# A hybrid attention and S5 block on one core: which weight matmuls stand beside which vector work, and the S5 scan on one engine

## Chip, core and metric

The kernel runs on one core of a Trainium2 chip. The metric is the device time of one execution in microseconds (us), as the median of the runs shown; the core is the only one, so its span is the execution but for what lies around it.

## What is computed

One decoder layer on 1024 tokens of width 1024, in float32:

```python
h = rmsnorm(x, norm_mix_pre)
q, k, v, u, g_attn, g_ssm = split(h @ w_in)     # 512, 128, 128, 512, 1024, 1024 columns
y_attn = sliding_window_attention(q, k, v, sinks, rel_bias) @ w_attn_branch
z = gelu(s5_ssm(u, lam, log_dt, b, c, d_skip))
z = z * sigmoid(z @ w_glu)
y_ssm = z @ w_ssm_branch
merged = sigmoid(g_attn) * y_attn + sigmoid(g_ssm) * y_ssm
x = x + rmsnorm(merged @ w_out, norm_mix_post)
h = rmsnorm(x, norm_mlp_pre)
x = x + rmsnorm(square(relu(h @ w_ff_in)) @ w_ff_out, norm_mlp_post)
```

The attention has 8 query heads on 2 key heads, blocks of 128 tokens with a band of 256 keys. The S5 part has 32 groups of 16 channels, each with a complex diagonal state of 64: `state = a * state + B u`, `y = Re(C state) + d u`, a scan along the sequence.

## The kernel before

**Number format.** Each float32 matmul is made of three: every operand is split into a high half (rounded by a copy on ScalarE) and a low half (`source - high`, on VectorE), and `mm3` (lines 184 to 190) issues high x high, high x low and low x high into one PSUM bank. One call of `proj_halves` (345) makes a 128x512 output tile from 8 such terms in two parts of 12 matmuls, with a `yield` between: such a part is what the text calls a step.

**Weights.** `WeightQueue` (45 to 121) loads raw weights in the order of the list in `weights` (209), as tiles of 128x2048 in two buffers, each two pieces of 1024. `pump` issues the high half of a piece (line 170), `flush` its low half (line 172) and the next loads. Three split pieces fit.

**Attention** (561) is a software pipeline over 16 half blocks in 20 iterations: iteration i issues the scores of half i (`a_scores`, with a maximum on VectorE), the softmax behind it (`a_softmax`: four Exp on ScalarE, line 523), transposes and splits for half i-2 (`a_trans`), the product with V for half i-3 (`a_pv`, copy at 556). At the end of an iteration come steps of a filler that keeps TensorE busy: one, and two in iterations 8, 11, 14, 15 and 16, so 24 in all. The filler is `u_proj` (813; 16 steps, u written to HBM as `ud`) and then the first 8 steps of `stage1` (956): for each of 16 tiles two steps of the gate g_attn, a sigmoid on ScalarE (972), one step of attention times w_attn_branch, their product on VectorE (985), written to HBM as `md`.

**Side work.** After attention the loop over the rest of stage1 calls `tick(11)` after each step (192 to 202): it plays pieces of a side generator, each with a cost, until the credit is spent or a piece says "wait". Side work is first `ssm_tables` (632): about a hundred small VectorE operations (recorded, so that all have line 42) for the exponentials and powers of a, the tables Vs (half of it on GpSimd), GW and four quarters of Q, with transposes (782) and small matmuls (765), written to HBM as `w1d`, `qd` and `kd`. Then `ssm` (833): `load1` reads `w1d` and `ud` back (lines 843, 846), `inputs` multiplies (864), the scan runs over state tiles F of 2x8x128, one half of the channels on VectorE and the other on GpSimd:

```python
v.tensor_tensor(out=t1, in0=src, in1=gb, op=ALU.mult)              # 877, src and dst: every 8th element
v.tensor_tensor(out=t2[:, 0], in0=src[:, 1], in1=g(2), op=ALU.mult)
v.tensor_tensor(out=t2[:, 1], in0=src[:, 0], in1=g(1), op=ALU.mult)
v.tensor_tensor(out=t1, in0=t1, in1=t2, op=ALU.add)
v.tensor_tensor(out=dst, in0=dst, in1=t1, op=ALU.add)              # 881
```

That is one `macc` (870); the scan has 18 (`scan`, 883). `stack` (895) moves halves of the partitions with three copies each (lines 902 to 904), `load2` (848) reads Q and T (from `qd`, `kd`; T by eight transfers, line 854), `outputs` (907) multiplies (916, 917), applies gelu (920 to 926) and writes z to HBM as `zd` in eight transfers per pair of tiles (932).

**Behind it.** `gates` (1023) makes the 16 tiles of sigmoid(g_ssm) into SBUF in 32 steps, still with ticks; before step 25 the side work is drained and `glu` (989) begins to load `zd`. Then glu's products, `stage2` (1036: branch times gates, `md` read back), `mix_out` (1120: w_out in three passes, norm) and `mlp`. The order is that of `run` (1294); nothing is reordered by a scheduler. Each engine takes its instructions in the order in which they are issued, and SP issues nearly all transfers.

Of the kernel before, what the change touches and what calls it, by code (L numbers as in the profile page):

```python
# [15 lines left out]
D = 1024  # L16
# [28 lines left out]
class WeightQueue:  # L45


    RAW, HL = 2, 3

    def __init__(self, blk, raws):  # L50
        self.blk = blk
        self.raws = raws
# [7 lines left out]
        self.halves = []  # L60

    def load(self, n=RAW):
        while self.in_use < n and self.n_load < len(self.raws):
            src, shape, own = self.raws[self.n_load]
            raw = self.blk.rawp.tile([P, 2048], F32, tag="raw", name="raw")
            n_pieces = src.shape[1] // 1024
            if self.n_load < 2:

                for i in range(n_pieces):
                    cs = slice(i * 1024, (i + 1) * 1024)  # L70
                    self.halves.append((raw[:, cs], src[:, cs]))
                self.load_half()
            else:
                self.blk.nc.sync.dma_start(out=raw[:, 0:n_pieces * 1024], in_=src)
            self.loaded.append((raw, [(i, shape, own[i]) for i in range(n_pieces)]))
            self.n_load += 1
            self.in_use += 1

    def load_half(self):
        out, src = self.halves.pop(0)  # L80
        self.blk.nc.sync.dma_start(out=out, in_=src)

    def pump(self, n=99):

        self.flush()
        while self.loaded and n:
            n -= 1
            raw, pieces = self.loaded[0]
            i, shape, own = pieces[0]
            if not own and self.live + self.ready_ring >= self.HL:  # L90
                break
            pieces.pop(0)
            last = not pieces
            if last:
                self.loaded.pop(0)
            src = raw[:, i * 1024:(i + 1) * 1024]
# [5 lines left out]
            self.pending.append((lo, last))  # L102

    def flush(self):
        for lo, last in self.pending:
            lo()
            self.in_use -= last
        self.pending = []
        self.load()
# [14 lines left out]
class Block:  # L124
    def __init__(self, ctx, tc, I, out):
# [3 lines left out]
        self.b16 = pool("b16", 6)  # L129
        self.r8 = pool("r8", 6)  # L130
        self.r4 = pool("r4", 3)
        self.t2 = pool("t2", 5)
        self.rawp = pool("raw", 2)
# [75 lines left out]
    def weights(self):  # L209
# [25 lines left out]
        return out + [ff2(NC - 1, keep(self.r, (0, 1)))]  # L235


    def consts(self):
# [8 lines left out]
        self.ones = c.tile([P, P], F32, name="ones")  # L247
# [38 lines left out]
    def x_load(self, q):  # L286
        nc, I = self.nc, self.I
        x, xt = self.r([2, D]), self.r([8, 256])
# [4 lines left out]
        if q == 0:  # L293
            nc.sync.dma_start(out=xt[:, 0:4], in_=I["xt"][q, :, 0:4])
            self.wq.load(1)
            self.wq.load_half()
# [90 lines left out]

    def qkv(self):
        nc = self.nc
        self.lo_eng = self.nc.gpsimd  # L390
        self.xq, self.xdiag = {}, {}
# [4 lines left out]
        self.wq.load_half()  # L396
# [13 lines left out]
        self.qa = (self.big([8, G, P]), self.big([8, G, P]))  # L410
# [8 lines left out]
        for qt in range(4):  # L419
# [6 lines left out]
            for n, (g, k, p) in enumerate(seq):  # L426
# [9 lines left out]
                if n == (32 if qt else 31) and qt + 1 < 4:  # L436
# [4 lines left out]
                    if qt == 2:  # L441
                        for g_ in range(3):
                            self.q_evac(early[g_], g_, 0)
            if qt == 3:
                self.lo_eng = None
            if qt == 1:
                early = ps
            if qt == 3:
                for g in range(3):
                    self.q_evac(ps[g], g, 1)  # L450
                    self.wq.done()
                    self.wq.pump()
        piece = self.wq.get()
        for h in range(2):
            ps = self.proj(piece, h)
            self.q_evac(ps, 3, h)
# [25 lines left out]
    def table_loads(self):  # L482
        self.tabA, self.tabB = self.r([2048]), self.r([2048])
# [77 lines left out]
    def attention(self, filler):  # L561
# [9 lines left out]
        for i in range(len(halves) + 4):  # L571
# [60 lines left out]
    def ssm_tables(self):  # L632
# [18 lines left out]
        self.GW = self.const.tile([P, 3, 11, 16], F32, name="GW")  # L651
# [61 lines left out]
        def powers(r_, i_, frm, k, to, m):  # L713
# [3 lines left out]
        powers(pr, pi, 1, 1, 2, 1)  # L717
        powers(pr, pi, 1, 2, 3, 2)
        powers(pr, pi, 1, 4, 5, 4)
# [4 lines left out]
        bb = lambda c: BB[:, c].unsqueeze(2).to_broadcast([P, 16, 8, 16])  # L724
        a = (pw4(0, 0, 16, 0, 8), pw4(1, 0, 16, 0, 8))
        T_ = [self.r([16, 8, 16]) for _ in range(2)]
        Vs = [self.r([16, 8, 16]) for _ in range(2)]
        self.cmul(nc.gpsimd, Vs[0], None, a, (bb(0), bb(1)), (T_[0], T_[0]))
        half = lambda v_, i: v_[:, 8 * i:8 * i + 8]
        for i in range(2):  # L730
            self.cmul(v, None, half(Vs[1], i), [half(x, i) for x in a], (half(bb(0), i), half(bb(1), i)), (None, half(T_[1], i)))
        yield from play(5)
# [4 lines left out]
        powers(gr, gi, 0, 0, 1, 1)  # L737
        powers(gr, gi, 0, 1, 2, 2)
        powers(gr, gi, 0, 3, 4, 4)
        for i in (8, 9, 10):  # L740
            powers(gr, gi, i - 1, i - 1, i, 1)
# [35 lines left out]
        def v_trans(ri, hf):  # L777
            pss = []
            for b in range(2):
                ps = self.ps()  # L780
                for k in range(4):
                    nc.tensor.transpose(ps[:, k * P:(k + 1) * P], Vs[ri][:, 8 * hf + 4 * b + k].rearrange("p t c -> p (t c)"), self.ident)
                pss.append(ps)
            return pss

        def v_out(ri, hf, pss):
            W = self.r([8, P])
            for b in range(2):
                nc.scalar.activation(out=W[:, 4 * b:4 * b + 4, :], in_=pss[b].rearrange("p (k s) -> p k s", k=4), func=AF.Copy)
            nc.sync.dma_start(out=self.w1d[hf, :, ri], in_=W)  # L790

        for q4 in range(4):
# [3 lines left out]
            Q = [self.q([4, 9, 16]) for _ in range(2)]  # L796
# [4 lines left out]
            yield from play(3)  # L801
# [6 lines left out]
            pss = v_trans(1 - q4 // 2, q4 % 2)  # L808
            yield "wait"
            kernel_out(q4, ps)  # L810
            v_out(1 - q4 // 2, q4 % 2, pss)

    def u_proj(self):
        nc = self.nc
        self.ud = self.dram.tile([SW, 8, P], F32, name="ud")
        for cp in range(2):
            ut = self.r([2, 8, P])
            for ci in range(2):
                piece = self.wq.get()
                for h in range(2):  # L820
                    for i, ps in enumerate(self.proj_halves(piece, h)):
                        if i == 1:
                            if h:
                                self.wq.done()
                                self.wq.pump()
                            nc.scalar.activation(out=ut[:, ci, :, 64 * h:64 * h + 64], in_=ps.rearrange("p (k j) -> p j k", j=8), func=AF.Copy)
                            if h:
                                c0 = cp * 256 + ci * P
                                nc.sync.dma_start(out=self.ud[c0:c0 + P], in_=ut[:, ci])
                        yield  # L830


    def ssm(self):
# [4 lines left out]
        xT, W1, F, T, Q = {}, {}, {}, {}, {}  # L838
# [17 lines left out]
        def inputs(hf):  # L856
            F[hf] = self.r([2, 8, P])
            nc.gpsimd.memset(F[hf][:, :, :, 0:1], 0.0)
# [537 lines left out]
```

## Time and profile before

| | us |
|---|---|
| three runs | 1364.54, 1367.31, 1368.42 (median 1367.31) |
| the profiled execution | 1364.96 |
| its span | 1363.2 |
| TensorE (PE) busy | 1293.4 (95%) |
| VectorE (DVE) busy | 778.8 (57%) |
| ScalarE (ACT) busy | 440.7 (32%) |
| GpSimd (POOL) busy | 209.7 (15%) |

How to read the rows: a row of busy time by stretch has the stretch, its length, then busy us and number of instructions of PE, PEld (weight loads), DVE, ACT and POOL, the granted TensorE clock (1.00 is 2.4 GHz, 0.50 is 1.2 GHz), the share of DMA time and GB/s. A row of a group has line, engine, operation, output<-input, shapes, number, then busy us, mean ns of one, and the idle time before them with what ended it. A row of the waits has who waited for whom, us in total, times, longest. A row of a timeline or of the chain has start, length, what. Matmuls overlap: two of 128x512 that follow each other start 0.227 us apart though each shows 0.39.

### The profile page before, as it was taken

The numbers are of one execution on the slowest core, as the hardware profiler recorded it, in microseconds if no ns is written. First come the engines' busy times: TensorE is split into PE (matmuls) and PEld (weight loads), VectorE is DVE, ScalarE is ACT, GpSimd is POOL, SyncE is SP. The second block draws the span as 40 slices with busy tenths as digits, with TensorE's granted clock in tenths as the row PEclk, the third lists the DMA queues.
The fourth block names the chain that finished last, engine by engine and source line by source line (L and its number), as shares of the span: only waits on it lengthen the run. The fifth ranks groups of instructions, "written<-read, shape, count | busy, mean of one in ns | idle before, by whom it ended". The sixth has DMA issues, their size and how long they took to land.

```text
span 1363.2 us, 15530 instructions
## 1 busy us (share of the span) xinstructions
PE 1293.4 (95%) x6144; PEld 1077.4 (79%) x6144; DVE 778.8 (57%) x1355; ACT 440.7 (32%) x774; POOL 209.7 (15%) x179
## 2 busy tenths in 40 slices
PE   8999999789749999998999999999999999999997
PEld 8988888677548778876788888888888888888886
DVE  5857869734982367467842554445544454445556
ACT  4557762212102253355543111211212111221132
POOL 1003214004970005152400000000000000000014
PEclk9999999898879999998999999999999999999999
DMA  8111021488105543455501010110011110110142
GB/s 340 48 62 63 32 93 57 130 199 171 47 31 120 127 155 124 154 186 185 186 31 62 31 62 32 62 62 31 33 61 62 49 45 31 63 62 31 49 180 96
DMA packets 42329, 124.22 MB, mean 91 GB/s; under 512 B 3856, under 2 KB 21008, under 8 KB 33552
## 3 DMA queue, kind: packets, MB, share of 16 engines
q1 hardware_dynamic: 42256, 123.22, 28.3%
q8 instruction: 48, 0.79, 0.2%
q14 instruction: 25, 0.20, 0.1%
HBM read 101.75 MB, written 21.46 MB: 90 GB/s over the span
## 4 chain that ended last, share of the span: by engine, by line
PE 73%; DVE 14%; ACT 5%; DMA 4%; issue 3%; SPq 1%; POOL 0%; DVEq 0%; ACTq 0%; POOLq 0%
PE ps L189 21%; PE ps L190 21%; PE ps L188 21%; DVE lo L172 2%; DMA r<-ud 1%; DVE r L42 1%; PE ps L1142 1%; PE ps L1143 1%; PE ps L1141 1%; DVE b L178 1%; DVE r L880 1%; ACT r L523 1%; DVE r L881 1%; DVE r L877 1%; DVE r L178 1%
## 5 line engine op out<-in xcount | busy, mean ns | idle before, releaser
L190 PE MATMUL ps<-b,lo 128*128 128x512 f32 x976 | 383.4, 393 | 17.7 <-DVE lo L172 17.7
L188 PE MATMUL ps<-b,hi 128*128 128x512 f32 x976 | 385.8, 395 | 1.3 <-ACT b L177 1.3
L189 PE MATMUL ps<-b,hi 128*128 128x512 f32 x976 | 383.1, 393 | 0.9 <-DVE b L178 0.9
L190 PEld LDWEIGHTS ps<-b,lo 128*128 128x128 f32 x976 | 185.1, 190 | 57.5 <-DVE lo L172 18.7
L170 ACT ACTIVATE hi<-raw 128x1024 fp32r<-128x1024 f32 x124 | 129.0, 1051 | 288.4 <-PE ps L190 236.9
L188 PEld LDWEIGHTS ps<-b,hi 128*128 128x128 f32 x976 | 185.4, 190 | 39.8 <-ACT b L177 1.9
L189 PEld LDWEIGHTS ps<-b,hi 128*128 128x128 f32 x976 | 185.0, 190 | 39.7 <-DVE b L178 1.8
L172 DVE TENSOR_TENSOR lo<-raw,hi 128x1024 fp32r<-128x1024 f32 x122 | 155.2, 1284 | 101.7 <-ACT hi L170 91.6
L1235 DVE TENSOR_TENSOR b<-b,ps 128x512 f32<-128x512 f32 x208 | 139.5, 686 | 98.9 <-PE ps L190 98.9
L190 PE MATMUL ps<-hi,r 128*128 128x512 f32 (+1 forms) x482 | 187.1, 388 | 0.0
L189 PE MATMUL ps<-lo,r 128*128 128x512 f32 (+1 forms) x482 | 187.1, 388 | 0.0
L188 PE MATMUL ps<-hi,r 128*128 128x512 f32 (+1 forms) x482 | 187.1, 388 | 0.0
L1176 DVE TENSOR_TENSOR t<-t 128x512 f32<-128x512 f32 x64 | 44.3, 692 | 163.9 <-ACT t L1175 163.9
L1289 POOL TENSOR_TENSOR t<-b,r 128x512 f32<-128x512 f32 (+1 forms) x17 | 20.5, 1227 | 663.8 <-DVE b L1286 663.8
L188 PEld LDWEIGHTS ps<-hi,r 128*128 128x128 f32 x482 | 90.5, 188 | 18.7
L189 PEld LDWEIGHTS ps<-lo,r 128*128 128x128 f32 x482 | 90.5, 188 | 18.7
L190 PEld LDWEIGHTS ps<-hi,r 128*128 128x128 f32 x482 | 90.5, 188 | 18.6
L1175 ACT ACTIVATE t<-ps 128x512 f32<-128x512 f32 x64 | 38.2, 597 | 189.7 <-PE ps L190 189.7
L178 DVE TENSOR_TENSOR r<-t,r 128x512 fp32r<-128x512 f32 x64 | 44.3, 693 | 44.8 <-ACT r L177 44.8
L177 ACT ACTIVATE r<-t 128x512 fp32r<-128x512 f32 x64 | 40.5, 633 | 49.9 <-DVE t L1176 48.9
L1142 PE MATMUL ps<-lo,b 128*128 128x512 f32 x128 | 51.5, 402 | 3.8 <-DVE lo L172 3.6
L1141 PE MATMUL ps<-hi,b 128*128 128x512 f32 x128 | 51.4, 402 | 1.7 <-DVE b L178 1.0
(198 smaller groups left out, 1550.1 us busy)
## 6 DMA issues: line engine op xcount, KB each, us to landing
raw<-in_ff_dram SPq DMA_DIRECT2D x32, 1024.0 KB, 4.9
raw<-in_wout_dram SPq DMA_DIRECT2D x12, 1024.0 KB, 4.9
raw<-in_win_dram SPq DMA_DIRECT2D x11, 1024.0 KB, 4.9
r<-in_x_dram SPq DMA_DIRECT2D x16, 512.0 KB, 7.3
md<-t SPq DMA_DIRECT2D x16, 256.0 KB, 2.0
raw<-in_wsb_dram SPq DMA_DIRECT2D x4, 1024.0 KB, 6.7
r<-md SPq DMA_DIRECT2D x4, 1024.0 KB, 8.2
x1d<-r SPq DMA_DIRECT2D x8, 512.0 KB, 6.0
```

The costliest lines, as they stand in the source:

```text
L170: nc.scalar.activation(out=hi, in_=src, func=AF.Copy)
L172: return (hi, lo), lambda: eng.tensor_tensor(out=lo, in0=src, in1=hi.bitcast(F32), op=ALU.subtract)
L177: nc.scalar.activation(out=hi, in_=src, func=AF.Copy)
L178: (eng or nc.vector).tensor_tensor(out=lo, in0=src, in1=hi.bitcast(F32), op=ALU.subtract)
L188: self.nc.tensor.matmul(ps, lhsT=ah, rhs=bh, start=first and i == 0, stop=False)
L189: self.nc.tensor.matmul(ps, lhsT=ah, rhs=bl, start=False, stop=False)
L190: self.nc.tensor.matmul(ps, lhsT=al, rhs=bh, start=False, stop=last and i == n - 1)
L1141: nc.tensor.matmul(ac[c], lhsT=a, rhs=wh[:, cs], start=k == 0, stop=False)
L1142: nc.tensor.matmul(ac[c], lhsT=a, rhs=wl[:, cs], start=False, stop=False)
L1175: nc.scalar.activation(out=rl, in_=ps, func=AF.Relu)
L1176: nc.vector.tensor_tensor(out=rl, in0=rl, in1=rl, op=ALU.mult)
L1235: nc.vector.tensor_tensor(out=a, in0=a, in1=ps, op=ALU.add)
```

## The change

In the order of the kernel:

- `weights`: the two slabs of u come first, the slabs of the SSM gates before those of stage1. Weights are loaded as pieces of 128x1024 in three buffers.
- `qkv`: the three pieces projected beside the norm of x are u's; the fourth u piece and the four q pieces follow with `tick(11)` after each of their 20 steps. Beside them the new generator `ssm_inputs_tables` plays the first part of the tables: the exponentials, powers, and Vs, now wholly on VectorE in two halves, with its transposes and `w1d`. Then `drain`.
- Attention has as filler 24 steps of `gates(range(6))` (12 tiles, whose sigmoids go to HBM as `sd`), then stage1; two steps in iterations 4 to 16, one in the others up to 18: 32 steps. From iteration 2 on `tick(8)` plays the second part of the tables (GW and Q). Then `drain`.
- The other 40 steps of stage1 have `ssm` beside them with `tick(11)`, then `drain`, with no step between. F is one tile of both halves, and one scan on VectorE does both (18 maccs of double width); all four `stack` steps are on VectorE.
- glu begins to load after that `drain`; `gates(range(6, 8))` makes the last four tiles beside it (8 steps).
- `stage2` reads `sd` back beside `md`. Pools: 7 large tiles for 6, 5 of 8 KB for 6, 3 raw for 2, 2 for Q; `ones` shares GW's tile.

```diff
-        win = lambda i: (I["win"][i], col, keep(self.r, (1,)) if i == 1 else none)
-        out = [win(i) for i in range(5)]
+        win = lambda i: (I["win"][i], col, keep(self.r, (1,)) if i == 4 else none)
+        out = [win(i) for i in (3, 4, 0, 1, 2)] + [win(9 + dp) for dp in range(3)]
         for dp in range(4):
             out += [(I["wab"][dp], half, none), win(5 + dp)]
-        out += [win(9 + dp) for dp in range(4)]
+        out.append(win(12))
...
+        self.side = [self.ssm_inputs_tables()]
+        for h, ps in self.proj_ticks(self.wq.get(), 11):
+            self.u_evac(ps, 3, h)
+        self.qa = (self.big([8, G, P]), self.big([8, G, P]))
+        for g in range(4):
+            piece = self.wq.get()
+            for h, ps in self.proj_ticks(piece, 11):
+                if h:
+                    self.wq.done()
+                    self.wq.pump()
+                self.q_evac(ps, g, h)
+        self.drain()
...
-            for _ in range(1 + (i in (8, 11, 14, 15, 16)) if i < 19 else 0):
+            for _ in range(1 + (4 <= i < 17) if i < 19 else 0):
                 next(filler, None)
+            if i >= 2:
+                self.tick(8)
...
+        for hf in range(2):
+            qs = slice(8 * hf, 8 * hf + 8)
...
+            self.cmul(v, Vs[0][:, qs], Vs[1][:, qs], a, (bb(0), bb(1)), (T_[:, 0], T_[:, 1]))
+            yield from play(6)
+            yield "wait"
...
-        def macc(hf, dst, src, i, n):
-
-            v = nc.gpsimd if hf else nc.vector
-            qs = slice(8 * hf, 8 * hf + 8)
-            g = lambda c: self.GW[:, c, i, qs].unsqueeze(2).to_broadcast([P, 8, n])
...
+        def macc(dst, src, i, n):
+
+            g = lambda c: self.GW[:, c, i].unsqueeze(2).to_broadcast([P, 16, n])
...
-                macc(hf, Fv[:, :, :, :, b], Fv[:, :, :, :, b - 1], 0, 16)
-                yield "wait"
+                macc(Fv[:, :, :, :, b], Fv[:, :, :, :, b - 1], 0, 16)
+                yield 14
...
         load2(0)
-        for step in (scan(1), stack(1)):
-            for _ in step:
-                pass
-        for _ in scan(0):
-            yield 8
+        yield from scan()
         yield from stack(0)
+        yield from stack(1)
         yield "wait"
         yield from outputs(0)
         load2(1)
...
-                self.nc.scalar.activation(out=self.sig[h][:, d], in_=ps, func=AF.Sigmoid)
+                sg = self.t([512])
+                nc.scalar.activation(out=sg, in_=ps, func=AF.Sigmoid)
+                nc.sync.dma_start(out=self.sd[d * P:(d + 1) * P, 512 * h:512 * h + 512], in_=sg)
...
             s1 = self.stage1()
-            self.attention(itertools.chain(self.u_proj(), s1))
-            self.table_loads()
-            self.side += [self.ssm_tables(), self.ssm()]
-            for i, _ in enumerate(s1):
+            self.side = [self.ssm_tables()]
+            self.attention(itertools.chain(self.gates(range(6)), s1))
+            self.drain()
+            self.side = [self.ssm()]
+            for _ in s1:
                 self.tick(11)
+            self.drain()
             glu = self.glu()
-            for i, g in enumerate(self.gates()):
-                self.tick(11)
-                if i == 24:
-                    self.drain()
-                    next(glu)
-                if i == 28:
+            next(glu)
+            for i, _ in enumerate(self.gates(range(6, 8))):
+                if i == 4:
                     next(glu)
```

## Rows read from the trace of the kernel before

**Rows 1.** Busy time by stretch: section A, then section B.

```profile
87.50:198.50 111.00, 110.39 (x604) 93.15 (x602) 84.94 (x263) 81.73 (x226) 28.63 (x16) 1.00 0.15 50
198.50:480.40 281.90, 237.16 (x1218) 196.99 (x1216) 171.41 (x323) 58.78 (x86) 89.33 (x105) 0.92 0.46 113
```

**Rows 2.** Busy time by stretch: slices of 20 us.

```profile
240.00:260.00 20.00, 12.32 (x60) 9.49 (x59) 15.47 (x61) 3.22 (x5) 0.19 (x1) 0.74 0.30 99
...
380.00:400.00 20.00, 2.79 (x14) 2.28 (x13) 19.45 (x27) 0.00 (x0) 18.67 (x27) 0.64 0.15 52
...
500.00:520.00 20.00, 18.32 (x73) 14.46 (x72) 12.96 (x15) 8.86 (x12) 4.64 (x4) 0.91 0.79 284
```

**Rows 3.** What TensorE waited for in section B.

```profile
PE ps L190 <- DVE lo L172: 17.7, 2, 10.0
PE ps L917 <- DVE r L904: 17.2, 1, 17.2
```

**Rows 4.** Timeline of TensorE: two matmuls of a step.

```profile
196.41 0.39 PE L188 MATMUL ps<-b,hi 128*128 128x512 f32 x1
196.64 0.39 PE L189 MATMUL ps<-b,hi 128*128 128x512 f32 x1
```

**Rows 5.** Groups of TensorE, 196 to 480 us: inputs, transposes of Vs, table matmuls.

```profile
L864 PE MATMUL ps<-r,r 128*64 128x128 f32 x128 | 10.3, 335 | 6.8 <-DMA r<-ud 5.2 <-DMA md<-t 1.6
L782 PE MATMUL ps<-ident,r 128*128 128x128 f32 x32 | 4.4, 280 | 0.0
L765 PE MATMUL ps<-r,r 128*32 128x128 f32 x64 | 2.7, 279 | 0.0
```

**Rows 6.** Groups of VectorE, 196 to 470 us.

```profile
L172 DVE TENSOR_TENSOR lo<-raw,hi 128x1024 fp32r<-128x1024 f32 x18 | 23.1, 1281 | 45.8 <-ACT hi L170 36.2 <-PE ps L782 9.6
L42 DVE TENSOR_TENSOR r<-r,r 128x576 f32<-128x576 f32 x24 | 17.3, 754 | 0.2
...
L881 DVE TENSOR_TENSOR r<-r,r 128x256 f32<-128x256 f32 x7 | 8.2, 1171 | 0.2
...
L42 DVE SCALAR_TENSOR_TENSOR r<-r 128x16 f32<-128x16 f32 x20 | 3.1, 174 | 0.3
...
L42 DVE TENSOR_TENSOR r<-r 128x256 f32<-128x256 f32 x6 | 2.1, 418 | 0.0
```

**Rows 7.** Busy time by stretch: iterations of attention with one step, then two.

```profile
135.25:140.77 5.52, 5.52 (x33) 4.79 (x32) 5.21 (x17) 4.17 (x14) 0.18 (x1) 1.00 0.35 105
146.30:155.04 8.74, 8.71 (x46) 6.95 (x44) 6.17 (x19) 6.89 (x18) 3.79 (x2) 1.00 0.06 24
```

**Rows 8.** Timeline of ScalarE at the first sigmoid, and a high half.

```profile
185.58 1.28 ACT L972 ACT_TABLE_LOAD   x1
186.88 0.60 ACT L972 ACTIVATE t<-ps 128x512 f32<-128x512 f32 x1
...
199.27 1.06 ACT L170 ACTIVATE hi<-raw 128x1024 fp32r<-128x1024 f32 x1
```

**Rows 9.** Chain that ended last: load1 (first issue, last landing), zd writes, load2(1).

```profile
292.22 0.28 SPq L843
...
313.18 6.08 DMA md<-t
...
428.41 0.30 SPq L932
...
432.14 0.38 SPq L850
...
436.44 9.21 DMA r<-kd
```

**Rows 10.** Groups of VectorE, 480 to 510 us: glu.

```profile
L178 DVE TENSOR_TENSOR b<-t,b 128x512 fp32r<-128x512 f32 x8 | 9.3, 1168 | 9.9 <-ACT b L177 9.9
L1018 DVE SCALAR_TENSOR_TENSOR t<-r,t 128x512 f32<-128x512 f32 x8 | 5.5, 686 | 1.7 <-ACT t L1017 1.5
```

**Rows 11.** Timeline of VectorE: first and last operation of an outputs tile.

```profile
403.59 0.43 DVE L921 TENSOR_SCALAR t<-t 128x512 f32<-128x512 f32 x1 [0.63 <-ACT t L920]
...
405.49 0.69 DVE L926 SCALAR_TENSOR_TENSOR r<-t,ps 128x512 f32<-128x512 f32 x1 [0.70 <-ACT t L924]
```

More of the change, by code (lines that the diff above doesn't have):

```diff
@@ L45 @@
 class WeightQueue:
-    RAW, HL = 2, 3
+    RAW, HL = 3, 3
     def __init__(self, blk, raws):
         self.blk = blk
-        self.raws = raws
+        self.raws = [(src[:, i * 1024:(i + 1) * 1024], shape, own[i])
+                     for src, shape, own in raws for i in range(src.shape[1] // 1024)]
         self.loaded = []
@@ L64, in load @@
             src, shape, own = self.raws[self.n_load]
[L65 to L75, printed above, removed]
+            raw = self.blk.rawp.tile([P, 1024], F32, tag="raw", name="raw")
+            self.blk.nc.sync.dma_start(out=raw, in_=src)
+            self.loaded.append((raw, shape, own))
             self.n_load += 1
             self.in_use += 1
-    def load_half(self):
-        out, src = self.halves.pop(0)
-        self.blk.nc.sync.dma_start(out=out, in_=src)
     def pump(self, n=99):
@@ L87, in pump @@
             n -= 1
-            raw, pieces = self.loaded[0]
-            i, shape, own = pieces[0]
+            src, shape, own = self.loaded[0]
             if not own and self.live + self.ready_ring >= self.HL:
                 break
[L92 to L96, printed above, removed]
+            self.loaded.pop(0)
             if len(shape) == 2:
@@ L101, in pump @@
             self.ready_ring += not own
[L102 removed]
+            self.pending.append(lo)
     def flush(self):
[L105 removed]
+        for lo in self.pending:
             lo()
[L107 removed]
+            self.in_use -= 1
         self.pending = []
@@ L234, in weights @@
             out += [ff1(c + 1), ff2(c)]
-        return out + [ff2(NC - 1, keep(self.r, (0, 1)))]
+        own = keep(self.r, (0,))[0], keep(self.big, (1,))[1]
+        return out + [ff2(NC - 1, own)]
     def consts(self):
@@ L386, in v_evac, with proj_ticks, u_evac @@
         self.split(pt.rearrange("p (n k d) -> p n k d", n=4, k=2), v[:, :, 0:4:2], v[:, :, 1:4:2])
+    def proj_ticks(self, piece, n):
+        for h in range(2):
+            for ps in self.proj_halves(piece, h):
+                self.tick(n)
+            yield h, ps
+    def u_evac(self, ps, g, h):
+        nc = self.nc
+        if g % 2 == 0 and h == 0:
+            self.ut[g // 2] = self.r([2, 8, P])
+        ut = self.ut[g // 2][:, g % 2]
+        nc.scalar.activation(out=ut[:, :, 64 * h:64 * h + 64], in_=ps.rearrange("p (k j) -> p j k", j=8), func=AF.Copy)
+        if h:
+            nc.sync.dma_start(out=self.ud[g * P:g * P + P], in_=ut)
     def qkv(self):
@@ L800, in ssm_tables @@
             v.tensor_tensor(out=Q[1], in0=Q[1], in1=T_, op=ALU.subtract)
-            yield from play(3)
+            yield from play(4)
             yield "wait"
@@ L934, in ssm @@
         load1(0)
+        yield "wait"
         load1(1)
+        F = self.big([2, 16, P], F32)
+        nc.gpsimd.memset(F[:, :, :, 0:1], 0.0)
         for _ in range(4):
@@ L938, in ssm @@
         for hf in range(2):
-            inputs(hf)
-            yield "wait"
+            yield from inputs(hf)
+        tmp = self.q([2, 512])
         load2(0)
-        for step in (scan(1), stack(1)):
-            for _ in step:
-                pass
-        for _ in scan(0):
-            yield 8
+        yield from scan()
         yield from stack(0)
+        yield from stack(1)
         yield "wait"
@@ L990, in glu @@
         nc = self.nc
-        zf = [self.r([2, L]) for _ in range(2)]
+        zf = self.big([2, 2, L], F32)
+        zf = [zf[:, c] for c in range(2)]
         zh = [self.r([2, L], F32R) for _ in range(2)]
@@ L1020, in glu, with gates @@
                     self.split(sg, hi, lo)
-    def gates(self):
-        self.sig = [self.big([8, 512], F32) for _ in range(2)]
-        for d in range(8):
+    def gates(self, ds):
+        nc = self.nc
+        for d in ds:
             piece = self.wq.get()
@@ L1038, in stage2 @@
         self.mT = []
-        ma, late = [], None
+        ma, sigs, late = [], [], None
         for h in range(2):
-            ma.append([self.r([4, 512]) for _ in range(2)])
+            sigs.append(self.big([8, 512], F32))
+            nc.sync.dma_start(out=sigs[h], in_=self.sd[:, 512 * h:512 * h + 512].rearrange("(k p) t -> p k t", p=P))
+            if h:
+                ma.append([self.r([4, 512]) for _ in range(2)])
+            else:
+                both = self.big([8, 512], F32)
+                ma.append([both[:, 0:4], both[:, 4:8]])
             for i in range(2):
```

173 lines of the change are left out of this document (79 added, 94 removed).

## The prediction, made before the changed kernel ran

> **What bounds the kernel now.** I read busy time by stretch first. What the change moves lies between the first score matmul (87.5 us) and the first matmul of glu (480.4), and I cut that in two [rows 1]: section A, 87.5 to 198.5 (attention, with weight matmuls between its own), and section B, 198.5 to 480.4 (rest of stage1, S5 tables, SSM, gates); together 392.9 us. In A TensorE is busy 110.4 of 111.0 us: it is the bound. In B it is busy 237 of 282 us at a mean clock of 0.92. Slices of 20 us [rows 2] say where its 45 idle us lie: 7.7 of them in 240:260, beside the tables, 17.2 in 380:400, at the scan's end, with a clock of 0.74 and 0.64. The list of what TensorE waited for names the ends: VectorE's low halves of weights (17.7 us in two waits), queued behind table work and scan, and the last copy after the scan (17.2 us) [rows 3]. So the prize is at most B's 45 us of idleness plus some 10 of low clock.
>
> My unit is one step: 12 matmuls of 128x512, which start 0.227 us apart [rows 4]: 2.72 us. Each `yield` of stage1, u_proj and gates is a step.
>
> **Moves that cost no TensorE time.** u's 16 steps leave A and go ahead of it (43.5 us); 24 gate steps leave B and fill A, so A gets 32 steps for 24 (+21.8 us). The 32 transposes of V (0.109 us each, 3.5) go ahead of A too, the 64 small table matmuls (2.4 us, near 0.6 for each of four groups) mostly into A [rows 5].
>
> **Ahead of A.** 83 small table operations (near 0.2 us each with their waits, 0.17 busy; six of 256 elements at 0.42) and 12 of 1024 now run on VectorE beside 20 steps (54 us). Before, GpSimd did part of the large ones at the same time; now it has none, and I price them as the 1024-element low halves, 1.28 [rows 6]. That is 18 + 15 us, with 16 q splits of 512 elements (near 0.69) and six low halves 52 of 54: hidden, barely. The transposes come two steps after what they read. I take 1 us, bounds 0 to 3. So ahead of A: 43.5 + 3.5 + 1 = 48.
>
> **Section A.** An iteration has 5.52 us of TensorE with one step and 8.74 with two (8.25 by count) [rows 7]. The new one has two steps in 13 iterations. ScalarE is the question. Exp and Sigmoid need different tables: a load of 1.28 us stands before the first sigmoid, and the sigmoid starts 0.02 us after it [rows 8]. Before, all sigmoids came after the last Exp. Now 12 of them fall between Exps, one an iteration from the fifth on: 24 more loads, 30.8 us. Per iteration: 4.17 (which includes one copy) + 2.57 + 0.6 for the sigmoid + half a high half of 1.06: near 7.9 of 8.25. VectorE has 5.2 + 0.6 (low half) + 1.5 (two table operations, 0.754 each [rows 6]) = 7.3. Both just fit as sums; but both queues are in order. Every second iteration the low half stands on VectorE ahead of table work and of the next scores, and waits for a high half that stands behind the Exps on ScalarE. Following the two queues through such a pair I get 18.4 us, against 16.5 of TensorE. Over the 5.5 pairs that is up to 10.6 us, of which softmax's lead of two iterations and the last iterations, with no loads, give back over half. I take +4, bounds 0 and 19 (the 11 iterations with loads ending 1.7 late each, as if no load were hidden behind a step's slack). A becomes 111 + 21.8 + 4 = 136.8.
>
> The Trainium skill (ScalarE: Activation LUTs, What ACT_TABLE_LOAD costs) has a switch cost about 2.66 us, half of it a drain behind the load. The rows show no such drain behind the load. By the Trainium skill's figure an iteration would have 10.6 us on ScalarE, and the sum would come out some 22 us higher.
>
> **Tables that are left over.** I followed the credits: 18 ticks of 8 play 47 small operations (six ticks), then five ticks for each quarter of Q. The fourth quarter is not begun when attention ends, and `drain` issues it with no step between. TensorE waits for VectorE to end the third quarter's last operations behind the last attention split (2.5 us), and for the fourth's six operations behind one kernel_out (6 x 0.754 + 0.6 = 5.2); with 1.2 of its own and an estimated 1.5 of low clock: 10.5 (bounds 6 and 14).
>
> **Section B, from the resumption of stage1 (0).** SP is free, so load1's 18 transfers go at once; before they took from 292.2 to 319.3, 27 us [rows 9]. Now inputs(0) comes at step 6 (16.3 us) and inputs(1) at step 10: nearly nothing is left of the 6.8 us that inputs waited. Thirteen steps and the inputs' matmuls (10 us) [rows 5] put the scan's start at 46.
>
> Its price is nowhere in the trace, since each macc ran beside GpSimd's: its last operation took 1.17 us for 256 elements [rows 6]. It reads and writes every eighth float. The nearest undisturbed row is glu's split, that also writes every eighth: 1.17 us for 512 elements, while a dense 512 takes 0.69 [rows 10]. So a full-width macc is 1.17 + 0.66 + 0.66 + 0.69 + 1.17 = 4.35 us strided, 2.91 if dense; all 18, the narrower ones scaled, 73 or 49 us. I take 73, for the stride is the same. The Trainium skill (SBUF — State Buffer, Door 1) has an access that leaves its 16-byte line pay a penalty; the split row agrees, and by a rule without it the sum would be 15 lower.
>
> Scan 73, stack(0) six copies of 512 elements (between the 0.43 of a one-source operation [rows 11] and the dense 0.69; 3), and what stage1 puts between on VectorE (12 steps carry four products of 0.69 and three low halves of 1.22: 0.54 a step, 24 steps, 13): the scan's copies end at 135. TensorE by itself is through its 40 steps and inputs at 119; it waits 16 us, about the old 17.
>
> Then nothing is left to cover the tail: `drain` issues it in one piece. stack(1) and stage1's last products 4.5; outputs(0), whose four tiles follow each other at 2.6 us from the first operation of one to that of the next (1.90 + 0.69 [rows 11]), 10.4; eight zd writes, 3.6 us on SP, which stand ahead of load2(1) there; load2(1) itself, from 432.1 to the last kd landing 445.6, 13.5 [rows 9]. That ends at 167, and TensorE, done with outputs(0) at 142, idles 25 us where before five steps and 3 us of wait covered the same loads. outputs(1) 5, and the eight remaining gate steps 21.8: 194. Beside them outputs(1) on VectorE (10.4), zd (5.6), zf (6.6) and the first split (2.2) end near 195. So B becomes 196.
>
> **Sum.** 48 + 136.8 + 10.5 + 196 = 391.3 against 392.9: 1.6 us less. What is taken away (waits on low halves, load1, half of the scan's contention) comes back as drains with no cover. I leave the rest at zero. Weights come as 512 KB instead of 1 MB with three buffers for two; the first lasting need is 2.7 us a piece in the last W_out pass, where about as many pieces are ahead as before. sig goes through HBM, 4 MB more to load at stage2: md's slice ran at 284 GB/s [rows 2], so the 8 MB take some 30 us, beginning in the middle of glu, and each quarter lands before its use; if not, 3 us. The profiled execution took 1364.96 us (span 1363.2); the median of the three runs is 1367.31, and I apply the difference to it: **1365.7 us**, no change within 0.3% (4.1 us, about what a measurement of this kernel can tell from none).
>
> **Rivals.**
> *The scan is not late* (faster). If the scan costs the dense price, or something between, it ends by 119, when TensorE gets there, and the 16 us wait goes: 1350. For it: no macc was ever seen alone, and half-width 256-element ones (1.17) cost as much as a strided 512. Against: the split row. If also the tail hides a few us, 1340.
> *ScalarE takes over attention* (slower). Place: iterations five to fifteen. Mechanism: two table loads an iteration. It decides once a pair of iterations on ScalarE and VectorE takes over 16.5 us by more than the end can give back. With the pair at 20 and nothing given back, 11 iterations cost 19 instead of 4: 1381. By the Trainium skill's price of a switch (the page named above) the same mechanism gives 11 x 2.4 = 26 us, 1388. For it: 7.9 of 8.25 us leaves no room in an in-order queue. Against: softmax is two iterations ahead of its use, and iterations with one step ran at TensorE's pace.
> *The tables do not get out of TensorE's way*: drain and tail each some us worse than followed by hand, about 1375; a weaker form of slower, not a mechanism of its own.
>
> **How the numbers follow.** My forecast (1358 to 1373) 0.45, the cheap scan (1340 to 1358) 0.27, the slow attention or tail (1373 to 1390) 0.28. Of the forecast's range about 0.13 lies beyond 0.3% faster and 0.05 beyond 0.3% slower. Range 1347 to 1384.
>
> **What would show it.** Right: a TensorE wait of about 15 us ended by VectorE at the scan's end, one of about 25 ended by kd, 5 to 8 at the end of attention; 24 table loads more on ScalarE; a 512-element macc operation at 1.17 us; no wait on the ud loads. Wrong: macc operations at 0.69, attention iterations over 9 us, or a kd wait under 10.

## The result, and the profile after

The changed kernel took 1381.97 us (median, 1380.46 to 1383.55, 4 runs) against 1365.92 of the kernel before beside it: a ratio of 1.0116, 95% interval 1.0094 to 1.0138. The forecast of no change was wrong; it is 16 us slower. The time lies in the stated range (1347 to 1384), but in the part that the prediction gave to slow attention or tail (1373 to 1390). The profiled execution has a span of 1380.6 us, 17.4 more than before.

First the stretches, which show where. This is busy time by stretch of the kernel after, in the order of the prediction's terms: ahead of attention, attention (from the first score matmul to the last matmul ahead of the wait for leftover tables), the leftover tables, the rest to the first matmul of glu.

```profile
87.50:135.57 48.07, 48.07 (x232) 40.16 (x231) 26.21 (x32) 20.54 (x33) 0.00 (x0) 1.00 0.34 110
135.57:293.02 157.45, 141.66 (x730) 113.16 (x729) 103.66 (x329) 116.58 (x255) 29.12 (x19) 0.98 0.19 56
293.02:304.40 11.38, 3.30 (x35) 1.55 (x34) 9.13 (x15) 2.28 (x3) 0.24 (x2) 0.72 0.37 80
304.40:499.10 194.70, 162.31 (x832) 133.70 (x833) 113.78 (x158) 38.45 (x56) 0.11 (x1) 0.90 0.55 124
```

| stretch | predicted | measured |
|---|---|---|
| ahead of attention | 48 | 48.07 |
| attention | 136.8 | 157.45 |
| leftover tables | 10.5 | 11.38 |
| to the first matmul of glu | 196 | 194.70 |
| sum (before: 392.9 [rows 1]) | 391.3 | 411.60 |

The sum grew by 18.7 us; what lies around these stretches took 1.3 less. The sum is 20.3 us over the forecast, and one row alone, attention, is 20.65 over. There TensorE was idle for 15.8 us, where it had been idle for 0.6 [rows 1], and no other engine was full: VectorE was busy 104 of 157 us, ScalarE 117. That points to engines that wait for each other in turn.

What TensorE waited for after, the largest (waiting engine and line, releaser: us in total, times, longest):

```profile
PE ps L917 <- DMA r<-kd: 24.6, 1, 24.6
PE ps L807 <- DVE qp L42: 8.1, 4, 2.9
PE ps L174 <- DVE lo L156: 7.8, 2, 6.4
PE ps L172 <- DVE t L815: 5.4, 1, 5.4
```

The second lies in the stretch of leftover tables, the third beside the scan; the last is the largest in attention. The waits on low halves fell from 17.7 to 7.8 us and the one at the scan's end (17.2) is gone [rows 3]; in their place stands the wait on `kd` at the tail, 24.6 us, which the prediction had at 25.

How attention loses time is seen on two queues. This is the timeline of ScalarE after (start, length, operation; in brackets the idle time before it and its releaser), five of the nine loads of Exp's table between 170 and 260 us, and of one iteration what stands behind its Exps up to the sigmoid:

```profile
172.05 1.28 ACT L538 ACT_TABLE_LOAD   x1 [3.26 <-DVE nm L535]
...
192.78 1.28 ACT L538 ACT_TABLE_LOAD   x1 [3.38 <-DVE nm L535]
...
201.65 1.28 ACT L538 ACT_TABLE_LOAD   x1 [1.39 <-DVE nm L535]
...
204.93 0.19 ACT L540 ACTIVATE es<-es 128x4 f32<-128x4 f32 x1
205.03 1.04 ACT L154 ACTIVATE hi<-raw 128x1024 fp32r<-128x1024 f32 x1
206.09 1.28 ACT L1036 ACT_TABLE_LOAD   x1
207.38 0.60 ACT L1036 ACTIVATE t<-ps 128x512 f32<-128x512 f32 x1
...
214.03 1.28 ACT L538 ACT_TABLE_LOAD   x1 [3.81 <-DVE nm L535]
...
255.93 1.28 ACT L538 ACT_TABLE_LOAD   x1 [4.17 <-DVE nm L535]
```

And VectorE in that iteration:

```profile
201.60 0.16 DVE L536 TENSOR_TENSOR es<-gn,nm 128x4 f32<-128x4 f32 x1
206.10 1.23 DVE L156 TENSOR_TENSOR lo<-raw,hi 128x1024 fp32r<-128x1024 f32 x1 [4.34 <-ACT hi L154]
207.24 0.75 DVE L42 TENSOR_TENSOR b<-b 128x576 f32<-128x576 f32 x1
...
208.80 0.42 DVE L525 CUSTOM_DVE_ANT_0 r<-ps,r 128x256 f32<-128x256 f32 x1
...
213.80 0.15 DVE L535 SCALAR_TENSOR_TENSOR nm<-mx,nsink 128x4 f32<-128x4 f32 x1
```

Read them together. ScalarE loads Exp's table, does its Exps and only then the high half of a weight piece (205.03). VectorE stands idle for 4.34 us in front of the low half of that piece, though tables and the next scores lie behind it in its queue. When the high half is there, VectorE does the low half, two table operations, scores and splits, and at 213.80 `nm`, for which ScalarE has waited 3.81 us. The engines work one after the other: 12.38 us from load to load, where TensorE needs 8.25. The other iteration of the pair (192.78 to 201.65) takes 8.87. The four pairs from 172.05 to 255.93 take 20.97 us each; by TensorE's count a pair is 16.5. Over the prediction's five and a half pairs, 4.47 us too much are 24.6 us; attention is 157.45 - 132.8 = 24.65 longer than its matmuls with 32 steps (111.0 + 21.8). That the two agree to a tenth is chance: some 1.2 us of the 24.65 are table matmuls that moved into attention (two of the four groups of near 0.6). Of the 24.65 us 15.8 show as idle time of TensorE. The other 8.9 stand in its busy time: the profile shows a matmul with 0.39 us, also where no other follows 0.227 behind it [rows 4], and the stretch ran at a clock of 0.98. They were not traced one by one.

At one place such a low half holds TensorE directly. A copy of table results (line 815) stands behind it on VectorE, and TensorE waits 5.4 us for that copy, the last row of the waits above. VectorE, then TensorE:

```profile
247.63 1.23 DVE L156 TENSOR_TENSOR lo<-raw,hi 128x1024 fp32r<-128x1024 f32 x1 [4.33 <-ACT hi L154]
248.89 0.29 DVE L815 COPY t<-ps 128x128 f32<-128x128 f32 x1
...
249.24 0.79 PE L172 MATMUL ps<-b,hi 128*128 128x512 f32 x1 [5.40 <-DVE t L815]
```

### The profile page after: what moved, and what is told of

Its sections match the earlier page's. It is cut to its first block, busy times and chain, and to the rows that moved or that the text cites. A ratio compares the mean times of both kernels' runs of the same rounds, so it can differ in the third digit from the quotient of the medians.

```text
span 1380.6 us, 15685 instructions
## 1 busy us (share of the span) xinstructions
PE 1300.3 (94%) x6144; PEld 1074.8 (78%) x6144; DVE 775.5 (56%) x1367; ACT 470.7 (34%) x797; POOL 120.7 (9%) x79
## 4 chain that ended last, share of the span: by engine, by line
PE 59%; DVE 4%; ACT 2%; DMA 1%; issue 1%; SPq 0%; DVEq 0%; ACTq 0%
PE ps L173 18%; PE ps L174 18%; PE ps L172 18%; PE ps L1152 1%; PE ps L1153 1%; PE ps L1151 1%; DVE lo L156 1%; DMA r<-kd 1%; ACT t L247 1%; DVE r L1090 1%; DMA r<-qd 0%; DVE b L162 0%; ACT b L161 0%; ACT r L1108 0%; PE ps L917 0%
## 5 line engine op out<-in xcount | busy, mean ns | idle before, releaser
L172 PEld LDWEIGHTS ps<-hi,r 128*128 128x128 f32 x482 | 90.5, 188 | 18.7
L173 PEld LDWEIGHTS ps<-lo,r 128*128 128x128 f32 x482 | 90.5, 188 | 18.7
```

The lines of the kernel that those rows point to most:

```text
L172: self.nc.tensor.matmul(ps, lhsT=ah, rhs=bh, start=first and i == 0, stop=False)
L173: self.nc.tensor.matmul(ps, lhsT=ah, rhs=bl, start=False, stop=False)
```

## The experiments

Three theories of attention's 24.65 us: the 24 table loads are the price (theory 1); the order of the two queues is (theory 2); the loads hide (theory 3). Each experiment is an edit of the kernel after. Attention is measured as above, "behind" is the stretch of leftover tables. The totals come from several sessions; the kernel before, timed in each, had medians of 1365.62 to 1366.94 us.

| edit | attention | behind | total (median) | ratio to the kernel before |
|---|---|---|---|---|
| none | 157.45 | 11.38 | 1381.97 | 1.0116 (1.0094 to 1.0138) |
| Tanh for Sigmoid | 139.02 | 11.82 | 1363.85 | 0.997 (0.9951 to 0.9989) |
| low halves on GpSimd | 146.17 | | 1373.25 | 1.0048 (1.003 to 1.0067) |
| no tables in attention | 150.34 | 31.69 | 1394.45 (one run) | |
| Tanh, low halves on GpSimd | 133.24 | | 1357.32 | 0.9918 (0.99 to 0.9936) |
| Tanh, 11 units of tables | 146.29 | 5.92 | 1364.05 | 0.998 (0.9962 to 0.9998) |
| filler ahead of softmax | 135.83 | | 1359.65 | 0.9949 (0.9931 to 0.9967) |

**Tanh for Sigmoid.** No part is left out: the half goes into glu's constant, the 1 into stage2's product.

```diff
-                nc.scalar.activation(out=sg, in_=ps, func=AF.Sigmoid)
+                nc.scalar.activation(out=sg, in_=ps, func=AF.Tanh, scale=0.5)
...
-                    nc.vector.scalar_tensor_tensor(out=sg, in0=part(zf[mp][:, mi]), scalar=0.5, in1=sg, op0=ALU.mult, op1=ALU.mult)
+                    nc.vector.scalar_tensor_tensor(out=sg, in0=part(zf[mp][:, mi]), scalar=0.25, in1=sg, op0=ALU.mult, op1=ALU.mult)
...
-                    nc.vector.tensor_tensor(out=sig[:, d], in0=sig[:, d], in1=ps, op=ALU.mult)
+                    nc.vector.scalar_tensor_tensor(out=sig[:, d], in0=sig[:, d], scalar=1.0, in1=ps, op0=ALU.add, op1=ALU.mult)
```

> The 12 gate tiles inside attention use Tanh of half the argument instead of Sigmoid (sigmoid is half of 1 + tanh; the 1 is added in stage2's product, the half goes into glu's constant). If Tanh shares a table with Exp, the 24 loads of 1.28 us in attention go. Theory 1 (the loads are the price): attention, 157.4 us from the first score matmul to the first matmul behind it, comes to within 5 us of the 132.8 that TensorE needs, so 135 to 138, and the whole to 1360 to 1363. Theory 2 (order: VectorE stands behind a low half whose high half stands behind the Exps on ScalarE, then tables, then the next scores): only one load an iteration with a weight piece is in that chain, a pair of iterations goes from about 21.2 to 18.5 us against 16.5 of TensorE, attention to 144, the whole to about 1369. Theory 3 (the loads hide in ScalarE's idle time): no change, 1382.

A group of ScalarE in attention with Tanh (line, engine, operation, number, then busy us, mean ns of one, and idle time before):

```profile
L538 ACT ACT_TABLE_LOAD x1 | 1.3, 1283 | 1.8 <-issue 1.8
```

It is the only load for Exp and the gates there: the twelve gates need none. The Trainium skill (ScalarE: Activation LUTs, Table sets: the hidden batching unit) lists Tanh in Exp's set; the row agrees. Attention fell by 18.4 us to 139.02, in no theory's range but nearest to theory 1, whose 138 and 1363 it passed by one. So the loads have a part in the loss; taken alone this run would have made them the whole cause.

**Low halves on GpSimd**, loads untouched (`lo_eng` is read when a piece is split):

```diff
         late = {}
+        self.lo_eng = self.nc.gpsimd
...
                 self.v_evac(self.v_late, 1)
+        self.lo_eng = None
```

> The low halves of weights in attention are made on GpSimd instead of VectorE; table loads stay. Theory 1 (the loads are the price): ScalarE's work of an iteration stays, attention stays within 5 us of 157 and the whole above 1376. Theory 2 (order): VectorE no longer stands 4.3 us before a low half and no longer does its 1.2 us in front of tables and scores; a pair goes from 21.2 to at most 18, attention to 135 to 142, the whole to 1360 to 1367. If GpSimd is so slow with the low half that TensorE waits for it, a wait on that line shows.

Attention fell by 11.3 us to 146.17: outside both ranges, and so is the whole, 1373.25. With every load in place theory 1 allowed 5. ScalarE was as busy as without the edit (116.55 us), so what went was waiting: before Exp's loads it waited 17.0 us for `nm`, where the kernel after has 28.9. TensorE did wait once for a low half on GpSimd, 1.7 us.

```profile
136.41:282.58 146.17, 138.72 (x730) 112.39 (x729) 95.51 (x323) 116.55 (x255) 43.21 (x26) 0.99 0.20 60
```

**No tables in attention.**

```diff
-            if i >= 2:
-                self.tick(8)
```

> No table work is played in attention; all of the second part of the tables is issued behind it with nothing beside it. Theory 2 (order): the 1.5 us of tables an iteration leave VectorE's chain, attention goes from 157 to 143 to 149 us; the rest behind attention grows from 11.4 to 35 to 45 us, the whole to 1392 to 1402. Theory 1 (the loads are the price): attention stays within 3 us of 155 (it loses 1.8 us of table matmuls), the whole 1405 or more.

```profile
135.27:285.61 150.34, 139.67 (x698) 112.39 (x697) 87.33 (x265) 117.19 (x256) 29.30 (x20) 0.98 0.16 50
285.61:317.30 31.69, 7.45 (x67) 3.53 (x66) 26.02 (x79) 1.65 (x2) 0.08 (x1) 0.59 0.31 71
```

Attention fell by 7.1 us, more than theory 1's bound and a little less than theory 2's; the stretch behind it, 31.69 us, is shorter than the 35 to 45 expected. The 20.3 us behind it cost more than was won. The tables belong in attention. Two groups of small matmuls, some 1.2 us, left attention with them; theory 2 would have the rest of the 7.1 as VectorE's part in the chain.

**Tanh and low halves on GpSimd together.** The two edits above.

> Tanh in the gates and the low halves of attention on GpSimd together. Each alone took 18.4 and 11.2 us from attention's 157.4. If both are links of one chain, what is left is TensorE's own work: attention 134.6 to 137, the whole 1360 to 1363. If they were separate costs the sum would be 29.6 us, 128 of attention, which is below what TensorE needs, so it can't be told from the chain by that alone; a rise above 139 us would say that GpSimd is now what is late.

```profile
135.96:269.20 133.24, 132.08 (x730) 111.87 (x729) 104.35 (x323) 86.23 (x231) 43.90 (x26) 1.00 0.21 66
```

133.24 us, of which TensorE is busy 132.08: attention is at TensorE's pace again, and it and the whole (1357.32) lie below the ranges expected. That 18.4 and 11.3 don't add up fits links of one chain, but does not show it: below TensorE's work there is nothing to win either way.

**Tanh and 11 units of tables an iteration** (`self.tick(11)` for `self.tick(8)`).

> Tanh in the gates, and 11 units of tables an iteration in attention instead of 8, so that the last quarters are played in attention. If attention has room on VectorE now, attention stays at 139 to 141 us, the stretch behind it falls from 11.4 to 3 to 6, and the whole is 1356 to 1360. If VectorE's chain is still at its limit, attention gets longer by what the stretch gets shorter: 1363 to 1366.

```profile
136.39:282.68 146.29, 138.60 (x746) 113.21 (x745) 111.05 (x336) 85.74 (x232) 29.24 (x20) 0.99 0.21 63
282.68:288.60 5.92, 1.95 (x19) 0.91 (x17) 4.60 (x7) 1.65 (x2) 0.00 (x0) 0.80 0.40 91
```

Attention got 7.3 us longer, the stretch behind it 5.9 shorter: nothing won. Without any load between Exps VectorE's place in the chain still sets the pace, though it is busy 111 of 146 us. So the chain can cost time without loads; how much of the 24.65 us it costs, this run does not say.

**Filler ahead of softmax.** All loads stay, Sigmoid stays, low halves stay on VectorE. Only the place in the queues changes: the filler's high half and sigmoid are issued before the Exps, and on VectorE its low half before `nm`.

```diff
+            for _ in range(1 + (4 <= i < 17) if i < 19 else 0):
+                next(filler, None)
             if i < 16:
                 n, kv = halves[i]
                 late["sm"] = self.a_softmax(n, kv, st[n])
                 next(late["sm"])
             late["old sm"] = late.pop("sm", iter(()))
-            for _ in range(1 + (4 <= i < 17) if i < 19 else 0):
-                next(filler, None)
```

> In each iteration of attention the filler's steps are issued before the softmax instead of behind it, so that the high half and the sigmoid stand ahead of the four Exps on ScalarE; the loads stay as many, Sigmoid stays, low halves stay on VectorE. If the place of the high half behind the Exps makes VectorE stand (4.3 us before the low half in every second iteration), the pair of iterations falls from 21.2 to 18 to 19.5 us, attention from 157.4 to 142 to 150, the whole to 1366 to 1375. If the loads alone set the pair, attention stays above 153 and the whole above 1377.

Busy time of attention with this edit:

```profile
135.12:270.95 135.83, 133.66 (x731) 113.03 (x729) 106.02 (x329) 120.32 (x257) 29.07 (x20) 0.99 0.22 65
```

Its loads, 26 in the two groups, where the kernel after has 25:

```profile
L538 ACT ACT_TABLE_LOAD x14 | 18.0, 1283 | 4.8 <-issue 2.8 <-DVE nm L535 1.8
L1036 ACT ACT_TABLE_LOAD x12 | 15.4, 1283 | 0.2
```

ScalarE's timeline at a weight piece:

```profile
196.90 1.28 ACT L538 ACT_TABLE_LOAD   x1 [0.90 <-DVE nm L535]
...
210.13 1.06 ACT L154 ACTIVATE hi<-raw 128x1024 fp32r<-128x1024 f32 x1
...
213.16 1.28 ACT L538 ACT_TABLE_LOAD   x1
```

VectorE's:

```profile
211.06 0.69 DVE L572 TENSOR_TENSOR t<-t,ps 64x512 f32<-64x512 f32 x1
211.78 1.23 DVE L156 TENSOR_TENSOR lo<-raw,hi 128x1024 fp32r<-128x1024 f32 x1
212.92 0.15 DVE L535 SCALAR_TENSOR_TENSOR nm<-mx,nsink 128x4 f32<-128x4 f32 x1
```

This decides it. The high half is done before VectorE comes to the low half, which has no bracket: no idle time. This pair takes 16.26 us (196.90 to 213.16), the five from 163.22 to 246.24 take 16.6 each, below the 18 expected. ScalarE waited 1.8 us for `nm` before Exp's loads, where the kernel after has 28.9:

```profile
L538 ACT ACT_TABLE_LOAD x13 | 16.7, 1283 | 30.7 <-DVE nm L535 28.9 <-issue 1.8
```

Attention fell by 21.6 us, 3.2 more than with Tanh, below the range that theory 2 gave. ScalarE is busy 120 of 136 us: 33 us of loads fit. Theory 1 falls, theory 3 too, since in the old order taking the loads away won 18.4 us; theory 2 stands, with the loads as links that make its chain longer. What costs is the old order together with the loads: without the loads it leaves attention at 139.02, and the loads in the new order leave it at 135.83. The edit moves high half, low half and sigmoid at once; which of the three moves counts most was not tried.

**The tail.** T of the second half loaded before the scan; only Q stays behind the first outputs (a second argument of 1 loads T alone, one of 0 Q alone).

```diff
         load2(0)
+        load2(1, 1)
         yield from scan()
...
-        load2(1)
+        load2(1, 0)
```

> Of the second half's load2, the eight transfers of T are issued with load2 of the first half, before the scan; only Q's transfer stays behind outputs of the first half. If the 24.6 us wait on kd at the tail is made by these transfers standing last on the queue, it shrinks by the eight issues and the last landing (about 13 us) to 8 to 13 us, ended by qd, and the whole comes to 1367 to 1371. If the wait is for the zd writes or for outputs themselves, it stays above 20 us, with another releaser, and the whole above 1378.

What SP issued at the tail in the kernel after (start, length of the group, number of issues):

```profile
444.56 8.69 SPq L933 DMA_DIRECT2D zd<-r  x16
453.35 0.38 SPq L857 DMA_DIRECT2D r<-qd  x1
453.83 6.67 SPq L861 DMA_DIRECT2D r<-kd  x8
```

With T loaded early:

```profile
PE ps L922 <- DMA r<-qd: 15.9, 1, 15.9
```

1372.37 us, 9.6 less; 1.0053 (1.0032 to 1.0074). The wait shrank by 8.7 us, not 13, and stayed above its range, as did the whole by 1.4: what was left is Q behind 16 `zd` writes. The next kernel, Tanh, T early and Q issued right behind the last matmul of the first outputs (`ahead`), ahead of the writes, which are kept back until then:

```diff
+                if gb == 3:
+                    ahead()
...
                 if gb % 2:
+                    writes.append((gb, zt))
```

> Three edits on the changed kernel: Tanh for the gates' Sigmoid, T of the second half loaded before the scan, and Q of the second half issued right behind the last matmul of the first outputs, ahead of the 16 zd writes. If the 15.9 us that were left on qd are the zd writes standing ahead of it on SP's queue, Q lands about 5 us after the last of those matmuls, the wait is 3 to 6 us, and the whole is 1363.9 - 9.5 - 11 = 1340 to 1346. If outputs on VectorE and ScalarE hold the tail, the wait goes to another line, and the whole stays above 1350.

```profile
PE ps L923 <- DMA r<-qd: 7.3, 1, 7.3
```

1344.66 us, 0.9825 (0.9808 to 0.9843): the total as expected. The wait is longer than expected; Q took 7.63 us from its issue to its landing, 4.85 with T early alone; why was not followed up.

**Low halves beside the scan on GpSimd**, which is idle in that stretch: `lo_eng` set from the end of attention to glu.

> In the stage1 steps beside the scan the low halves of weights are made on GpSimd, which is idle there; all else as in the changed kernel. If the two waits on low halves (7.8 us) are the scan's pieces standing ahead of them on VectorE, they go and VectorE is about 10 us less busy: 1373 to 1376. If GpSimd at the same memory slows the scan (in the kernel before a half-width operation took as long beside GpSimd as a full one takes now), the scan of 80 us gets longer by 10 us or more, TensorE waits for its end, and the whole is 1380 or more.

Groups of VectorE in the kernel after, a scan operation of 224 elements:

```profile
L881 DVE TENSOR_TENSOR r<-b,GW 128x224 f32<-128x224 f32 x1 | 0.6, 593 | 0.0
```

VectorE beside GpSimd in the experiment:

```profile
396.48 2.63 DVE L881 TENSOR_TENSOR r<-b,GW 128x224 f32<-128x224 f32 x1
399.03 2.67 DVE L882 TENSOR_TENSOR r<-b,GW 128x224 f32<-128x224 f32 x1
```

GpSimd at that time:

```profile
396.25 5.07 POOL L156 TENSOR_TENSOR lo<-raw,hi 128x1024 fp32r<-128x1024 f32 x2 [13.30 <-ACT hi L154]
```

What TensorE waited for:

```profile
PE ps L918 <- DVE b L905: 12.2, 1, 12.2
```

1390.58 us, 8.6 slower than without the edit. An operation of 0.59 us took 2.63 while GpSimd's ran, and the scan's end came 12.2 us too late for TensorE.

**Versions that beat both kernels.** Tanh, GpSimd for attention's low halves, and the tail's edits; then 11 units of tables; then the inputs in four pieces for eight and a cost of 17 for a piece of the scan.

> Tanh in the gates, low halves of attention on GpSimd, T loaded before the scan and Q ahead of the zd writes together. If attention's chain and the tail are independent, the sum of what each took: 1357.3 (the first two) less 19.2 (the tail's two edits, 1363.9 to 1344.7): 1336 to 1340. If a shorter attention only makes the tail wait longer, above 1343.

> As best_a, with 11 units of tables an iteration for 8. With VectorE freed of the low halves there should now be room: attention stays at 133 to 136 us, the stretch behind it falls from about 11 to 6, the whole to 1331 to 1336. If VectorE is still at its limit, as it was with Tanh alone, no change against best_a: 1336 to 1340.

> As best_b, with the inputs of the scan in four pieces instead of eight, so that the scan starts four steps (11 us) earlier, and a cost of 17 for each of its 18 pieces instead of 14. If the 7.8 us of waits on low halves beside the scan come from its pieces being issued faster than VectorE does them, they shrink to 0 to 4, the whole to 3 to 8 us below best_b. If VectorE is simply full until the scan's end, the waits stay or go to the scan's end, and the whole is within 2 us of best_b.

They took 1338.73 (0.9799, 0.9772 to 0.9826), 1333.94 (0.9762, 0.9735 to 0.9788) and 1329.59 us (0.9733, 0.9706 to 0.9761), each in its range. The second shows that the tables fit once the low halves are gone from VectorE (attention 134.29 us, behind it 5.90), which they did not with Tanh alone. The third, what TensorE waited for:

```profile
PE ps L925 <- DMA r<-qd: 5.2, 1, 5.2
PE ps L875 <- DMA r<-ud: 4.3, 1, 4.3
...
PE ps L174 <- DVE lo L156: 2.6, 2, 2.2
```

The waits on low halves fell from 7.8 to 2.6 us, and a part comes back as a wait for `ud`, presumably since the inputs are asked for earlier. The order of the filler ahead of softmax was not tried together with the tail's edits.

## Why the prediction was wrong

The step that failed is in "Section A": "Following the two queues through such a pair I get 18.4 us", "of which softmax's lead of two iterations and the last iterations, with no loads, give back over half. I take +4, bounds 0 and 19". The mechanism was the one named there, the low half standing on VectorE for a high half behind the Exps. Two sizes were off: a pair took 20.97 us, and nothing was given back. The term was 24.65 (some 1.2 of it table matmuls that the sum for attention left out), above its upper bound, and the prediction's own sign of being wrong, iterations over 9 us, came with 12.38. Why nothing came back is read from the code and not tried by a run: softmax's lead is in the order in which TensorE takes its matmuls, not in time; the queues are in order, so an iteration that is late makes the later ones late by as much, unless a later one has time to spare.

- *Ahead of attention*, 48 against 48.07: right as a sum. TensorE was never idle there, so the 1 us of waiting in the term did not come. The 1024-element operations on VectorE alone took 1.22 us, where the prediction had the 1.28 of a low half [rows 6].
- *Leftover tables*, 10.5 against 11.38: right.
- *The scan's price*: right, at the strided end. The rows below are the groups of VectorE in the kernel after. A full macc is 4.26 us against 4.35 (1132 + 631 + 630 + 693 + 1170 ns; the second cross product, line 882, has the 630). The copies of stack(0) ended at 434.83, 130.4 us after stage1's resumption, against 135.

```profile
L884 DVE TENSOR_TENSOR b<-b,r 128x512 f32<-128x512 f32 x7 | 8.2, 1170 | 0.2
...
L880 DVE TENSOR_TENSOR r<-b,GW 128x512 f32<-128x512 f32 x7 | 7.9, 1132 | 1.1 <-ACT b L872 1.0
...
L883 DVE TENSOR_TENSOR r<-r 128x512 f32<-128x512 f32 x7 | 4.8, 693 | 0.2
...
L881 DVE TENSOR_TENSOR r<-b,GW 128x256 f32<-128x256 f32 x7 | 4.4, 631 | 0.0
```

- *The wait of 16 us at the scan's end*: it did not come. TensorE, forecast to be through its own work at 119, came to outputs 132.0 us after the resumption (436.39), when those copies were done, so that no wait of outputs is ended by VectorE. On the way it had waited 7.8 us for low halves behind pieces of the scan, and the stretch ran at a clock of 0.90. That the term's sum holds, 196 against 194.70, is partly luck: 32.4 us of TensorE's idle time for 41 forecast, and 162.3 us of busy time for 155.
- *The uncovered tail*, 25 against 24.6: right, and the two tail experiments took 19.2 us out of it (1363.85 to 1344.66).
- *The table loads*: 24 more, as forecast (25 for Exp and the gates in attention after, one for Exp before). The Trainium skill (ScalarE: Activation LUTs, What ACT_TABLE_LOAD costs) puts a drain of 1.38 us beside the load's 1.28; the trace does not show it: the load is 1.28 us and the sigmoid starts 0.01 us behind it (206.09, 207.38).
- *The rivals*: "ScalarE takes over attention" named the place, and its pair at 20 us with nothing given back was near. That its 1381 meets 1381.97 is partly luck: it priced attention's loss at 19, not 24.65, while the last stretch and what lies around the stretches came out 1.3 us lower each. Its name is half right. The loads lengthen the chain, and without them 18.4 us went; but ScalarE had 41 us idle there, and with the loads in another order attention ran at TensorE's pace.

## What to carry to other kernels

In a pipeline over in-order queues the sum of each engine's work says only that it could fit; the chain through the queues says whether it does. Where an operation waits on one engine for another's, ask what stands ahead of that other one in its queue, and issue the producer before the long work rather than behind it: here that was worth 21.6 us, more than taking nearly all table loads away. A removed cost that speeds a kernel up need not be the whole cause, nor its removal the best cure: only the run that kept the loads and changed the order told.

## What the runs showed of the hardware

GpSimd and VectorE did not work side by side in the scan's stretch: with low halves on GpSimd, seven operations of the scan that met a low half on GpSimd took 2.6 to 3.3 us, about the length of GpSimd's operation, whatever their own (0.59 to 1.17 us). It would also explain why half-width operations of the scan took 1.17 us beside GpSimd [rows 6], as long as full-width ones take alone; that was not tried by itself. The Trainium skill (SBUF — State Buffer, SBUF: two separate sides) calls the port an exclusive lock, held for a whole instruction; the rows of the experiment agree. In attention the same move helped. There GpSimd's low half fell into time in which VectorE stood idle for ScalarE anyway: in the run with that edit alone GpSimd worked from 203.52 to 205.91, and VectorE waited 2.97 us up to 205.87.
